# Cumulated decays by chunk in DRAM, a product over its factor, and a second buffer for the backward rows

## The chip, the cores and the metric

The kernel runs on one core of one Trainium2 chip. Its time is the device time of one execution in microseconds: 3032.32 us, median of 3 runs from 3030.61 to 3033.17.

## What is computed

Two network blocks on a sequence of 1024 tokens of width 1024, all in float32. The first is a Mamba-2 block that runs in both directions, with a Fourier mixer beside it; the second is attention and a mixture of experts. The change touches only the chunked scan of the first block. The reference for one direction, with 4 groups of 6 heads, 64 channels a head, a state of 128 and 8 chunks of 128 tokens:

```python
a_cum = jnp.cumsum(a, axis=-1)                 # per head, within a chunk
lmat = jnp.exp(segsum(a))
cb = jnp.einsum('bclgn,bcsgn->bgcls', cc, bc)
y_diag = jnp.einsum('bgcls,bgrcls,bcsgrp->bclgrp', cb, lmat, xc)
decay_states = jnp.exp(a_cum[..., -1:] - a_cum)
states = jnp.einsum('bcsgn,bgrcs,bcsgrp->bcgrpn', bc, decay_states, xc)
...
new_states = jnp.einsum('bgrzc,bcgrpn->bzgrpn', decay_chunk, states)
y_off = jnp.einsum('bclgn,bcgrpn,bgrcl->bclgrp', cc, prev_states, jnp.exp(a_cum))
y = (y_diag + y_off).reshape(bsz, length, g, r, p)
```

The scan runs once forward and once over the flipped sequence, and both results are added.

## The kernel before

Early on, the 48 cumulated decays (24 heads, two directions) of all 1024 tokens are laid out with heads on partitions in `prs` [48, 1024]. ScalarE's queue writes them to DRAM as `pr_d`, and their exponentials as `ep_d` (L418 to L420). From there SyncE's queue later loads single heads' rows broadcast over partitions.

`ssd_group(g)` does one group of heads, chunk by chunk. For chunk step i it calls `off` for both directions and `diag`:

- `off(dr, i)`: TensorE multiplies the carried state H with C into `pof`; VectorE multiplies that by the broadcast decays `er` (two DMAs of 64 partitions x 3 rows x 128 tokens, L757) into `tm` (L763); GpSimd adds `tm` to the output `xs` (L766). Then H is brought forward: `pst` on TensorE (L771), a multiply on GpSimd (L773), an add on VectorE (L775).
- `diag(c)`: `pcb` = B C on TensorE, masked into `cbm`. Two broadcast loads of 6 rows x 128 tokens to 128 partitions, `pf` with the forward rows (L787) and `rb` with the backward rows (L788; the trace calls its tile `rbw`). For each of the 6 heads ScalarE adds a column to `rb` (L791) and VectorE makes the smaller of the two exponents into `pf` (the STT of L792). ScalarE takes the exponential (L794), VectorE the products `W` with the masks (L797), TensorE the products `pd` (L804), and VectorE adds `pd` to `xs` (L807). That add ends a chunk.

Tiles of the pool `wk` have two buffers unless told otherwise. `rb` has one (`bufs=1`), `pf` two. Four PSUM banks (`ps`) serve `pof`, `pst`, `pcb` and `pd`.

The order on each engine is not the order of the code. A planner places instructions by priorities and its own estimates of their durations. The projections of the next group (`plain_tile`, L350, whose PSUM tiles are `pxz`) have a lower priority (`high_priority(-FILL)`) and fill TensorE where the planner sees it wait; in group 3 output products (`out_group`) do that. Each engine executes its own list strictly in order, and a DMA is issued when its turn on its queue has come and its waits are over.

Of the kernel before, what the change touches and what calls it, by code (L numbers as in the profile page):

```python
# [8 lines left out]
F32 = mybir.dt.float32  # L9
# [5 lines left out]
ALU = mybir.AluOpType  # L15
# [4 lines left out]
P = 128  # L20
D = 1024
NT = 8
# [155 lines left out]
def block1(tc, A, x1_d, mod_d, second):  # L178


    nc = tc.nc
    es0 = ExitStack()
    con = es0.enter_context(tc.tile_pool(name="b1c", bufs=1))
    dpool = es0.enter_context(tc.tile_pool(name="b1d", bufs=1, space=DRAM))
# [1 line left out]
    z_d = [dpool.tile([P, 1024], F32, name=f"z{m}") for m in range(16)]  # L186
    u_d = [dpool.tile([P, 1024], F32, name=f"u{m}") for m in range(4)]
    y_d = [dpool.tile([P, 1024], F32, name=f"y{m}") for m in range(16)]
    pr_d = dpool.tile([48, 1024], F32, name="pr_d")
    ep_d = dpool.tile([48, 1024], F32, name="ep_d")  # L190
    hs_d = [[dpool.tile([P, 384], F32, name=f"hs{dr}{g}") for g in range(4)] for dr in range(2)]
    gate_d = dpool.tile([2, 512], F32, name="gate_d")

# [33 lines left out]
    with ExitStack() as e1:  # L227
# [3 lines left out]
        wk = e1.enter_context(tc.tile_pool(name="b1wk", bufs=2))  # L231
# [130 lines left out]
    with ExitStack() as e1:  # L362
# [49 lines left out]
        prs = sp.tile([48, 1024], F32, name="prs")  # L412
        for half in range(2):
# [1 line left out]
            for t in range(4):  # L415
                nc.tensor.transpose(pq[:48, t * P:(t + 1) * P], prt[:, half * 4 + t, :], ident)
            nc.scalar.copy(prs[:, half * 512:half * 512 + 512], pq[:48])
        nc.scalar.dma_start(pr_d, prs)  # L418
        nc.scalar.activation(prs, prs, AF.Exp)
        nc.scalar.dma_start(ep_d, prs)  # L420
        edt.close()


# [264 lines left out]
    with ExitStack() as e2:  # L688
        gp = e2.enter_context(tc.tile_pool(name="b1g", bufs=1, reuse_waits="tile"))
        wk = e2.enter_context(tc.tile_pool(name="b1k", bufs=2, reuse_waits="tile"))  # L690
        psa = e2.enter_context(tc.tile_pool(name="b1qa", bufs=1, space=PSUM))

        def ps1(name):
            return psa.tile([P, 512], F32, name=name, tag="ps", bufs=4)
# [9 lines left out]
        def ssd_group(g):  # L704
# [10 lines left out]
            def by_head(t_):  # L715
                return t_.rearrange("p (h d) -> p h d", d=64)
# [10 lines left out]
            def scaled(c, w, tag, eng):  # L727
                o = wk.tile([P, 6, 64], F32, name=f"xw{g}{c}{tag}", tag="xw", bufs=4)
                eng.tensor_tensor(out=o, in0=by_head(xtok[:, c, :]), in1=w.unsqueeze(2).to_broadcast([P, 6, 64]),
                                  op=ALU.mult)  # L730
                return o
# [18 lines left out]
            def off(dr, i):  # L750

                c = i if dr == 0 else NT - 1 - i
                hs = slice(dr * 24 + 6 * g, dr * 24 + 6 * g + 6)
                er = wk.tile([P, 3, P], F32, name=f"er{g}{dr}{i}", tag=f"er{dr}")
                for q in range(2):
                    rows = ep_d[hs, c * P:(c + 1) * P].rearrange("(j q) t -> q j t", q=2)[q:q + 1]
                    nc.sync.dma_start(er[64 * q:64 * q + 64], rows.broadcast_to([64, 3, P]))  # L757
                po = ps1(f"pof{g}{dr}{c}")
                for j in range(3):
                    nc.tensor.matmul(po[:, j * P:(j + 1) * P], H[dr][:, j * P:(j + 1) * P], ct[:, c * P:(c + 1) * P],  # L760
                                     start=True, stop=True)
                tm = wk.tile([P, 3, P], F32, name=f"tm{g}{dr}{c}", tag="tm")
                nc.vector.tensor_tensor(out=tm, in0=po[:, :384].rearrange("p (j t) -> p j t", j=3),  # L763
                                        in1=er, op=ALU.mult)
                y = xs[:, :, c * P:(c + 1) * P]
                nc.gpsimd.tensor_tensor(out=y, in0=y, in1=tm, op=ALU.add)  # L766
                if i == NT - 1:
                    return
                xw = scaled(c, wS[:, c, hs], f"s{dr}", nc.vector)
                pst = ps1(f"pst{g}{dr}{c}")  # L770
                nc.tensor.matmul(pst[:, :384], btok[:, c, :], xw.rearrange("p h d -> p (h d)"), start=True, stop=True)  # L771
                nx = wk.tile([P, 384], F32, name=f"H{g}{dr}{c}", tag=f"H{dr}")
                nc.gpsimd.tensor_tensor(out=by_head(nx), in0=by_head(H[dr]),  # L773
                                        in1=expT[:, c, hs].unsqueeze(2).to_broadcast([P, 6, 64]), op=ALU.mult)
                nc.vector.tensor_tensor(out=nx, in0=pst[:, :384], in1=nx, op=ALU.add)  # L775
                H[dr] = nx

            def diag(c):
                cs = slice(c * P, (c + 1) * P)
                pcb = ps1(f"pcb{g}{c}")  # L780
                nc.tensor.matmul(pcb[:, :P], bt[:, cs], ct[:, cs], start=True, stop=True)
                cbm = wk.tile([P, 2, P], F32, name=f"cbm{g}{c}", tag="cbm")
                nc.vector.tensor_tensor(out=cbm[:, 0, :], in0=pcb[:, :P], in1=upper, op=ALU.mult)
                nc.vector.tensor_tensor(out=cbm[:, 1, :], in0=pcb[:, :P], in1=lower, op=ALU.mult)
                pf = wk.tile([P, 6, P], F32, name=f"pf{g}{c}", tag="pf")
                rb = wk.tile([P, 6, P], F32, name=f"rbw{g}{c}", tag="rbw", bufs=1)
                nc.sync.dma_start(pf, pr_d[6 * g:6 * g + 6, cs].unsqueeze(0).to_broadcast([P, 6, P]))  # L787
                nc.sync.dma_start(rb, pr_d[24 + 6 * g:30 + 6 * g, cs].unsqueeze(0).to_broadcast([P, 6, P]))  # L788
                for hh in range(6):
                    h = 6 * g + hh  # L790
                    nc.scalar.activation(rb[:, hh, :], rb[:, hh, :], AF.Identity, bias=nrt[:, c, h:h + 1])  # L791
                    nc.vector.scalar_tensor_tensor(pf[:, hh, :], pf[:, hh, :], prt[:, c, h:h + 1], rb[:, hh, :],  # L792
                                                   op0=ALU.subtract, op1=ALU.min)
                nc.scalar.activation(pf, pf, AF.Exp)  # L794
                W = wk.tile([P, 2, 6, P], F32, name=f"W{g}{c}", tag="W")
                for dr in range(2):
                    nc.vector.tensor_tensor(out=W[:, dr], in0=pf, in1=cbm[:, dr, :].unsqueeze(1).to_broadcast([P, 6, P]),  # L797
                                            op=ALU.mult)
                xd = [scaled(c, dtt[:, c, dr * 24 + 6 * g:dr * 24 + 6 * g + 6], f"d{dr}", nc.vector) for dr in range(2)]
                pd = ps1(f"pd{g}{c}")  # L800
                for j in range(3):
                    for dr in range(2):
                        for q in range(2):
                            nc.tensor.matmul(pd[64 * q:64 * q + 64, j * P:(j + 1) * P], xd[dr][:, 2 * j + q, :],  # L804
                                             W[:, dr, 2 * j + q, :], start=(dr == 0), stop=(dr == 1))
                y = xs[:, :, cs]
                nc.vector.tensor_tensor(out=y, in0=pd[:, :384].rearrange("p (j t) -> p j t", j=3), in1=y, op=ALU.add)  # L807

            for i in range(NT):
                if 1 < i < 5:  # L810
                    load_z(i - 2)
                off(0, i)
                off(1, i)
                diag(i)
# [45 lines left out]
    with ExitStack() as e2:  # L860
# [18 lines left out]
        for k in (2, 3):  # L879
            zt[k] = []  # L880
            for n in range(2):
                h, l = (second.h_tile(s, 4 + 2 * (k - 2) + n).rearrange("p k t -> p (k t)") for s in "hl")
# [15 lines left out]
        wk = e2.enter_context(tc.tile_pool(name="b1fin", bufs=4, side="right", reuse_waits="tile"))  # L898
# [1317 lines left out]
def whole(tc, A, out):  # L2216

    nc = tc.nc
    with ExitStack() as e:
        dp = e.enter_context(tc.tile_pool(name="wd", bufs=1, space=DRAM))  # L2220
        x1_d = dp.tile([1024, D], F32, name="x1_d")
        mod_d = dp.tile([12, 512], F32, name="mod_d")
        with tc.tile_pool(name="wz", bufs=1) as zp:
            z = zp.tile([P, D], F32, name="zero_rows")
            nc.gpsimd.memset(z, 0.0)
            nc.gpsimd.dma_start(out[1024:], z)
        second = Second(tc, A, x1_d, mod_d, out, {})
        block1(tc, A, x1_d, mod_d, second)
        with tc.using_default_side("right"):
            second.projections()  # L2230
            attention(second)
            merge(second)
            experts(second)
# [17 lines left out]
```

## Time and profile before

| | |
|---|---|
| median of 3 runs | 3032.32 us |
| the profiled execution | 3029.96 us |
| its span, first to last instruction | 3028.2 us |
| TensorE, VectorE, ScalarE, GpSimd busy | 2710.3, 2115.3, 1484.0, 590.6 us |
| granted TensorE clock, mean | 0.954 |
| the scan (er first issued, last add into xs) | 420.9 to 956.3 us |

The first 95 us hold norms and modulation, up to 410 us the projections and the convolution run, then the scan of four groups to about 960 us. Output products, Fourier part, attention and experts follow, the experts at 370 GB/s of weights. In the scan no engine is full: TensorE is busy for 448.3 of the 550 us from 410 to 960, VectorE for 336.4, ScalarE for 216.3, GpSimd for 160.2. Chunk k of group g carries the number gk in tile names, as `W15`; `er104` is group 1, direction 0, step 4.

### The profile page before, as it was taken

The page shows a single profiled execution, that of the slowest core. Times are in us where ns is not written, and L with a number is a line of the kernel's source. Part 1 is how long each engine was busy: PE and PEld are TensorE (multiplying, and loading weights), DVE is VectorE, ACT ScalarE, POOL GpSimd, SP SyncE. Part 2 cuts the span into 40 slices and gives each one's busy share as a digit, 9 for nine tenths or more (in the row PEclk, how much of TensorE's full clock was granted, in tenths as well). Part 3 has the DMA queues.
Part 4 walks back from the last instruction along what each step waited for, and adds up shares of the span by engine and source line. Part 5 has one row for each costly group of instructions (what it writes and reads, how often), then busy time and mean ns, then how long its engine had stood idle before and what let it go on. Part 6 is the DMA issues. An engine that isn't in the chain of part 4 may idle for free. (4 is left out here: it accounts for less than half of the span.)

```text
span 3028.2 us, 39461 instructions
## 1 busy us (share of the span) xinstructions
PE 2710.3 (90%) x14016; PEld 2135.6 (71%) x14016; DVE 2115.3 (70%) x3664; ACT 1484.0 (49%) x2401; POOL 590.6 (20%) x449
## 2 busy tenths in 40 slices
PE   5999988879787999688999999999999699999997
PEld 2767766657665777566877877778778588777775
DVE  6777747676566656777667745655446899999996
ACT  4433324435342232555766635654221477777774
POOL 2000003222225422421213100000124212112111
PEclk9999998999888999798999999999999799999999
DMA  5265346666545424211233355100445699999995
GB/s 215 78 252 213 125 154 144 192 142 180 137 124 169 154 70 137 91 46 35 81 108 123 111 173 185 47 29 27 139 145 193 230 376 372 368 371 372 373 368 193
DMA packets 270819, 533.08 MB, mean 176 GB/s; under 512 B 25446, under 2 KB 135654, under 8 KB 266524
## 3 DMA queue, kind: packets, MB, share of 16 engines
q1 hardware_dynamic: 202112, 411.98, 40.2%
q10 hardware_dynamic: 56844, 84.99, 7.9%
q0 software_dynamic: 11664, 33.57, 4.5%
q8 instruction: 111, 1.82, 0.2%
q14 instruction: 88, 0.72, 0.1%
HBM read 449.25 MB, written 90.11 MB: 178 GB/s over the span
## 5 line engine op out<-in xcount | busy, mean ns | idle before, releaser
L2057 DVE TENSOR_TENSOR wh<-we,wh 128x1024 fp32r<-128x1024 f32 x390 | 456.2, 1218 | 16.4 <-ACT wh L2054 9.4
L2054 ACT CAST wh<-we 128x1024 fp32r<-128x1024 f32 x396 | 396.6, 1051 | 91.0 <-DMA we<-in_w_ex 28.7
L446 DVE SCALAR_TENSOR_TENSOR acc<-img,cvw,acc 128x945 f32<-128x945 f32 (+2 forms) x160 | 193.1, 1219 | 52.6 <-ACT acc L437 50.6
L2093 PE MATMUL pae<-wh,xle 128*128 128x512 f32 x528 | 207.5, 394 | 5.9 <-DVE xle L2078 5.9
L2091 PE MATMUL pae<-wh,xhe 128*128 128x512 f32 x528 | 210.7, 399 | 2.2 <-ACT xhe L2077 2.2
L2092 PE MATMUL pae<-wh,xhe 128*128 128x512 f32 x528 | 209.8, 397 | 0.1
L792 DVE SCALAR_TENSOR_TENSOR pf<-pf,prt,rbw 128x128 f32<-128x128 f32 x192 | 77.1, 445 | 122.5 <-ACT rbw L791 87.9
L791 ACT ACTIVATE rbw<-rbw,nrt 128x128 f32<-128x128 f32 x192 | 60.0, 390 | 179.0 <-DMA rbw<-pr_d 178.0
L773 POOL TENSOR_TENSOR H<-H,expT 128x384 f32<-128x384 f32 x56 | 54.8, 980 | 455.3 <-DMA H<-hs 348.0
L2114 PE MATMUL pye<-wh,ghe 128*128 128x512 f32 x264 | 106.9, 405 | 21.8 <-ACT ghe L2106 21.8
L350 PE MATMUL pxz<-hTh,w_h 128*128 128x512 f32 x320 | 115.2, 431 | 9.0 <-ACT w_h L143 5.3
L2068 POOL DMA_INDIRECT xg<-h_d,gidx x33 | 35.9, 1089 | 443.3 <-PE pxe L2074 426.2
L350 PE MATMUL pxz<-hTh,w_l 128*128 128x512 f32 x320 | 115.8, 435 | 7.2 <-DVE w_l L144 7.2
L2093 PEld LDWEIGHTS pae<-wh,xle 128*128 128x128 f32 x528 | 99.8, 189 | 27.0 <-DVE xle L2078 6.7
L766 POOL TENSOR_TENSOR xs<-xs,tm 128x384 f32<-128x384 f32 x64 | 74.1, 1161 | 218.6 <-DVE tm L763 218.3
L2091 PEld LDWEIGHTS pae<-wh,xhe 128*128 128x128 f32 x528 | 99.9, 189 | 23.1 <-ACT xhe L2077 2.8
L2092 PEld LDWEIGHTS pae<-wh,xhe 128*128 128x128 f32 x528 | 100.0, 189 | 22.1 <-DVE wh L2057 1.9
L350 PE MATMUL pxz<-hTl,w_h 128*128 128x512 f32 x320 | 111.1, 426 | 0.0
L350 PE MATMUL pxc<-hTh,w_h 128*128 128x512 f32 x320 | 105.8, 404 | 2.6 <-ACT acc L437 2.6
L588 PE MATMUL po<-woh,yh 128*128 128x512 f32 x224 | 92.7, 414 | 14.5 <-DVE acc L593 10.7
L2116 PE MATMUL pye<-wh,gle 128*128 128x512 f32 x264 | 103.7, 393 | 0.1
L2115 PE MATMUL pye<-wh,ghe 128*128 128x512 f32 x264 | 103.1, 391 | 0.0
(911 smaller groups left out, 7687.2 us busy)
## 6 DMA issues: line engine op xcount, KB each, us to landing
we<-in_w_ex SPq DMA_DIRECT2D x396, 512.0 KB
ad_w<-in_ada_w SPq DMA_DIRECT2D x24, 1024.0 KB
wr<-in_w_in SPq DMA_DIRECT2D x40, 512.0 KB
er<-ep_d SPq DMA_DIRECT2D x128, 96.0 KB
pf<-pr_d SPq DMA_DIRECT2D x32, 384.0 KB
rbw<-pr_d SPq DMA_DIRECT2D x32, 384.0 KB
xbc<-acc ACTq DMA_DIRECT2D x20, 512.0 KB
wada<-in_w_ada SPq DMA_DIRECT2D x8, 1024.0 KB
```

The lines of the kernel that those rows point to most:

```text
L350: nc.tensor.matmul(px[j], wt[:, k, :mc], ht[:, k, 512 * j:512 * j + 512], start=(k == 0 and n == 0), stop=(k == KD - 1 and n == 2))
L446: nc.vector.scalar_tensor_tensor(o, img[:, r0 + dy:r1 + dy, c0 + dx:c1_ + dx], cvw[:, m, tap:tap + 1], o, op0=ALU.mult, op1=ALU.add)
L588: nc.tensor.matmul(po, yh[:, ts_], wh, start=(k == 0), stop=False)
L792: nc.vector.scalar_tensor_tensor(pf[:, hh, :], pf[:, hh, :], prt[:, c, h:h + 1], rb[:, hh, :], op0=ALU.subtract, op1=ALU.min)
L2054: last["h"] = nc.scalar.copy(h, raw)
L2057: eng.tensor_tensor(out=l, in0=raw, in1=h.bitcast(F32), op=ALU.subtract)
L2091: nc.tensor.matmul(pa, xh[:, kk, :], h[:, cs], start=(kk == 0), stop=False)
L2092: nc.tensor.matmul(pa, xh[:, kk, :], l[:, cs], start=False, stop=False)
L2093: last["mm"] = nc.tensor.matmul(pa, xl[:, kk, :], h[:, cs], start=False, stop=(kk == KD - 1))
L2114: nc.tensor.matmul(o, gh[:, kk, :], h[:, cs], start=(kk == 0), stop=False)
L2115: nc.tensor.matmul(o, gh[:, kk, :], l[:, cs], start=False, stop=False)
L2116: nc.tensor.matmul(o, gl_[:, kk, :], h[:, cs], start=False, stop=(kk == 3))
```

## The change

`pr_d` and `ep_d` are laid out by chunk, [8, 48 x 128], so that the 6 rows of a group, or the 3 that one `er` DMA takes, are one contiguous run. `pr_d` is still written by one DMA, `ep_d` by six (the heads of each parity and pair apart). The loads become two-dimensional patterns; that of the backward rows comes first. The product of L763 is written over `er`, and `tm` is gone. `rb` has the pool's two buffers.

```diff
-    pr_d = dpool.tile([48, 1024], F32, name="pr_d")
-    ep_d = dpool.tile([48, 1024], F32, name="ep_d")
+    pr_d = dpool.tile([NT, 48 * P], F32, name="pr_d")
+    ep_d = dpool.tile([NT, 48 * P], F32, name="ep_d")
...
-        nc.scalar.dma_start(pr_d, prs)
+        nc.scalar.dma_start(pr_d.rearrange("c (p t) -> p c t", t=P), prs.rearrange("p (c t) -> p c t", t=P))
         nc.scalar.activation(prs, prs, AF.Exp)
-        nc.scalar.dma_start(ep_d, prs)
+        for q in range(2):
+            for j in range(3):
+                nc.scalar.dma_start(ep_d.rearrange("c (d s t) -> s d c t", s=6, t=P)[3 * q + j],
+                                    prs[2 * j + q::6, :].rearrange("p (c t) -> p c t", t=P))
...
-                er = wk.tile([P, 3, P], F32, name=f"er{g}{dr}{i}", tag=f"er{dr}")
+                er = wk.tile([P, 3 * P], F32, name=f"er{g}{dr}{i}", tag=f"er{dr}")
                 for q in range(2):
-                    rows = ep_d[hs, c * P:(c + 1) * P].rearrange("(j q) t -> q j t", q=2)[q:q + 1]
-                    nc.sync.dma_start(er[64 * q:64 * q + 64], rows.broadcast_to([64, 3, P]))
+                    lo = (2 * (4 * dr + g) + q) * 3 * P
+                    nc.sync.dma_start(er[64 * q:64 * q + 64], ep_d[c:c + 1, lo:lo + 3 * P].broadcast_to([64, 3 * P]))
...
-                tm = wk.tile([P, 3, P], F32, name=f"tm{g}{dr}{c}", tag="tm")
-                nc.vector.tensor_tensor(out=tm, in0=po[:, :384].rearrange("p (j t) -> p j t", j=3),
-                                        in1=er, op=ALU.mult)
+                nc.vector.tensor_tensor(out=er, in0=po[:, :384], in1=er, op=ALU.mult)
                 y = xs[:, :, c * P:(c + 1) * P]
-                nc.gpsimd.tensor_tensor(out=y, in0=y, in1=tm, op=ALU.add)
+                nc.gpsimd.tensor_tensor(out=y, in0=y, in1=er.rearrange("p (j t) -> p j t", j=3), op=ALU.add)
...
-                rb = wk.tile([P, 6, P], F32, name=f"rbw{g}{c}", tag="rbw", bufs=1)
-                nc.sync.dma_start(pf, pr_d[6 * g:6 * g + 6, cs].unsqueeze(0).to_broadcast([P, 6, P]))
-                nc.sync.dma_start(rb, pr_d[24 + 6 * g:30 + 6 * g, cs].unsqueeze(0).to_broadcast([P, 6, P]))
+                rb = wk.tile([P, 6, P], F32, name=f"rbw{g}{c}", tag="rbw")
+                for dr, dst in ((1, rb), (0, pf)):
+                    lo = (24 * dr + 6 * g) * P
+                    nc.sync.dma_start(dst.rearrange("p h t -> p (h t)"), pr_d[c:c + 1, lo:lo + 6 * P].broadcast_to([P, 6 * P]))
```

The planner makes another order of the whole scan out of it. Three places:

SyncE in group 1, before (rbw14 is the load of the backward rows of chunk 4, er105 and er115 are the decays of chunk step 5):

```order
L787 DMA pf13_4990<-pr_d_127 128x6x128
L757 DMA er104_5030<-ep_d_128 64x3x128 x2
L788 DMA rbw13_4991<-pr_d_127 128x6x128
L757 DMA er114_5047<-ep_d_128 64x3x128 x2
L787 DMA pf14_5069<-pr_d_127 128x6x128
L757 DMA er105_5107<-ep_d_128 64x3x128 x2
L757 DMA er115_5124<-ep_d_128 64x3x128 x2
L788 DMA rbw14_5070<-pr_d_127 128x6x128
L787 DMA pf15_5146<-pr_d_127 128x6x128
L757 DMA er106_5184<-ep_d_128 64x3x128 x2
L757 DMA er116_5201<-ep_d_128 64x3x128 x2
L788 DMA rbw15_5147<-pr_d_127 128x6x128
```

And in the change:

```order
L791 DMA rbw14_5049<-pr_d_127 128x768
L791 DMA pf14_5048<-pr_d_127 128x768
L791 DMA rbw15_5124<-pr_d_127 128x768
L761 DMA er105_5086<-ep_d_128 64x384 x2
L224 DMA wr7_3560<-in_w_in 128x1024
L761 DMA er115_5102<-ep_d_128 64x384 x2
L791 DMA pf15_5123<-pr_d_127 128x768
L761 DMA er106_5161<-ep_d_128 64x384 x2
L761 DMA er116_5177<-ep_d_128 64x384 x2
L791 DMA rbw16_5199<-pr_d_127 128x768
```

Before, rbw15 came behind the er rows of chunk 6; now it comes ahead of those of chunk 5.

VectorE around W15, the two mask products of chunk 5 in group 1, before:

```order
L797 TENSOR_TENSOR W15_5163<-pf15_5146,cbm15_5143 128x768 x2
L729 TENSOR_TENSOR xw11s1_5211<-xtok1_4651,wS_155 128x384
L763 TENSOR_TENSOR tm106_5191<-pof106_5187,er106_5184 128x384
L792 SCALAR_TENSOR_TENSOR pf16_5223<-pf16_5223,prt_157,rbw16_5224 128x128 x3
L807 TENSOR_TENSOR xs1_4643<-pd15_5170,xs1_4643 128x3x128
L775 TENSOR_TENSOR H106_5198<-pst106_5196,H106_5198 128x384
```

And in the change:

```order
L800 TENSOR_TENSOR W15_5140<-pf15_5123,cbm15_5120 128x768 x2
L795 SCALAR_TENSOR_TENSOR pf17_5259<-pf17_5259,prt_157,rbw17_5260 128x128 x6
L144 TENSOR_TENSOR w14_l_4325<-wr14_4322,w14_h_4324 128x1024
L810 TENSOR_TENSOR xs1_4632<-pd15_5147,xs1_4632 128x3x128
L733 TENSOR_TENSOR xw16d0_5218<-xtok1_4640,dtt_156 128x384
L733 TENSOR_TENSOR xw16d1_5220<-xtok1_4640,dtt_156 128x384
L766 TENSOR_TENSOR er106_5161<-pof106_5164,er106_5161 128x384
L777 TENSOR_TENSOR H106_5174<-pst106_5172,H106_5174 128x384
```

The six STT behind W15 were those of the next chunk, in pieces; now they are those of the chunk after next, all in front of the add that ends chunk 5.

TensorE between pcb03 and pd03 (chunk 3 of group 0), before; pxz121 and pxz120 are a projection of the next group, and 24 such rows stand there in all:

```order
L771 MATMUL pst014_3954<-xw04s1_3952,btok0_3626 128x384
L781 MATMUL pcb03_3959<-ct0_3619,bt0_3618 128x128
L350 MATMUL pxz121_3252<-hTh_414,w12_h_3247 128x512
L350 MATMUL pxz120_3251<-hTl_415,w12_h_3247 128x512
L350 MATMUL pxz121_3252<-hTl_415,w12_h_3247 128x512
L350 MATMUL pxz120_3251<-hTh_414,w12_l_3248 128x512
```

And in the change:

```order
L773 MATMUL pst014_3951<-xw04s1_3949,btok0_3631 128x384
L783 MATMUL pcb03_3956<-ct0_3624,bt0_3623 128x128
L807 MATMUL pd03_3985<-W03_3978,xw03d0_3981 64x128 x2
L764 MATMUL pof004_4004<-ct0_3624,H003_3937 128x128 x3
L807 MATMUL pd03_3985<-W03_3978,xw03d1_3983 64x128 x2
```

The 24 filling rows are gone from this place and stand later.

## Rows read from the trace of the kernel before

**Rows 1.** Busy time by stretch: engine busy us (instructions), granted clock, DMA share, GB/s
```profile
260.00:410.00 150.00, 144.73 (x733) 109.11 (x733) 115.99 (x117) 53.93 (x92) 0.00 (x0) 0.97 0.41 150
...
410.00:960.00 550.00, 448.30 (x2483) 342.98 (x2483) 336.35 (x648) 216.31 (x414) 160.15 (x139) 0.90 0.59 154
...
460.00:560.00 100.00, 82.86 (x499) 63.27 (x500) 75.44 (x143) 39.80 (x79) 31.40 (x30) 0.93 0.61 136
```

**Rows 2.** Waits of 440 to 960 us: who for whom, total us, times, longest
```profile
ACT rbw L791 <- DMA rbw<-pr_d: 178.0, 29, 11.9
...
DVE pf L792 <- ACT rbw L791: 87.9, 21, 12.8
...
PE pd L804 <- DVE W L797: 27.4, 15, 5.2
...
DVE pf L792 <- DMA pf<-pr_d: 26.1, 4, 7.7
...
PE pst L771 <- DVE xs L807: 14.4, 5, 7.1
...
PE ptx L722 <- ACT btok L725: 12.5, 1, 12.5
```

**Rows 3.** SyncE's timeline: start us, us, line, DMA, count
```profile
445.14 1.13 SPq L788 DMA_DIRECT2D rbw<-pr_d  x1
...
608.38 0.37 SPq L788 DMA_DIRECT2D rbw<-pr_d  x1
...
621.90 0.36 SPq L788 DMA_DIRECT2D rbw<-pr_d  x1
...
874.32 0.36 SPq L787 DMA_DIRECT2D pf<-pr_d  x1
```

**Rows 4.** ScalarE's timeline: start us, us, [idle before, and who ended it]
```profile
455.24 1.28 ACT L791 ACTIVATE rbw<-rbw,nrt 128x128 f32<-128x128 f32 x4 [10.61 <-DMA rbw<-pr_d]
...
459.37 0.48 ACT L724 COPY xtok<-ptx 128x384 f32<-128x384 f32 x1 [0.45 <-ACT oz L701]
...
616.62 1.86 ACT L791 ACTIVATE rbw<-rbw,nrt 128x128 f32<-128x128 f32 x6 [7.36 <-DMA rbw<-pr_d]
...
766.14 1.86 ACT L791 ACTIVATE rbw<-rbw,nrt 128x128 f32<-128x128 f32 x6 [11.90 <-DMA rbw<-pr_d]
```

**Rows 5.** VectorE's timeline, the same columns
```profile
485.65 0.55 DVE L807 TENSOR_TENSOR xs<-pd,xs 128x384 f32<-128x384 f32 x1
...
559.14 0.56 DVE L807 TENSOR_TENSOR xs<-pd,xs 128x384 f32<-128x384 f32 x1 [3.49 <-PE pd L804]
...
620.44 1.44 DVE L792 SCALAR_TENSOR_TENSOR pf<-pf,prt,rbw 128x128 f32<-128x128 f32 x3
...
858.74 0.55 DVE L807 TENSOR_TENSOR xs<-pd,xs 128x384 f32<-128x384 f32 x1
881.22 1.66 DVE L792 SCALAR_TENSOR_TENSOR pf<-pf,prt,rbw 128x128 f32<-128x128 f32 x6 [6.92 <-DMA pf<-pr_d]
...
923.30 0.55 DVE L807 TENSOR_TENSOR xs<-pd,xs 128x384 f32<-128x384 f32 x1
```

**Rows 6.** TensorE's timeline, the same columns
```profile
460.07 0.90 PE L722 MATMUL ptx<-ident,xs 128*128 128x128 f32 x3 [12.53 <-ACT btok L725]
...
609.98 1.05 PE L350 MATMUL pxz<-hTh,w_h 128*128 128x512 f32 x2
...
613.84 0.44 PE L804 MATMUL pd<-W,xw12d 128*64 128x128 f32 x4
...
618.84 0.63 PE L350 MATMUL pxz<-hTh,w_l 128*128 128x512 f32 x2
...
622.02 0.61 PE L350 MATMUL pxz<-hTh,w_h 128*128 128x512 f32 x2
```

**Rows 7.** Instructions of single tensors: ns min/median/max, first and last start us
```profile
L757 SPq DMA_DIRECT2D er<-ep_d x128: 573/603/3272, 420.9 to 926.9; - x128
...
L420 ACTq DMA_DIRECT2D ep_d<-prs x1: 315/315/315, 106.1 to 106.1; - x1
```

## Prediction

> **What bounds the kernel now.** I read the table of stretches first. From 410 to 960 us, where the chunked scan runs, TensorE is busy for 448 of 550 us, VectorE for 336, and the DMA engines are 0.59 busy [rows 1]. Neither compute engine is full, so the waits were next. TensorE's idle time there is mostly VectorE's lateness (the product W 27.4 us, the add into xs 14.4) and one wait of 12.5 us at the start [rows 2]. VectorE in turn waits 87.9 us for ScalarE's rbw and 26.1 us for pf's DMA, and ScalarE waits 178.0 us for rbw's DMA [rows 2]. So the timelines of one chunk came third: SyncE issues rbw at 608.38, ScalarE starts on it at 616.62, VectorE's last read of it ends at 620.44 + 1.44 = 621.88, and SyncE issues the next rbw at 621.90 [rows 3, 4, 5]. With one buffer this is a closed loop: 8.2 us of flight and 5.3 us of use, 13.5 us a chunk. The adds into xs that end each chunk show that the loop paces the light chunks: six intervals from 485.65 to 559.14, 12.25 us each [rows 5]. VectorE's work is shorter: 75.4 us in 460 to 560 us, which holds the eight chunks of group 0, is 9.4 us each [rows 1].
>
> TensorE's own work of a chunk is about 4.8 us: from 613.84 to 618.84 with one filling matmul among it. A filling matmul (the projections of L350) costs 0.227 us at 2.4 GHz (14 from 618.84 to 622.02) and nearly twice that at 1.2 GHz (two in 1.05 us at 609.98, after a pause of TensorE) [rows 6]. So a chunk with some 28 of them is bound by TensorE rather than VectorE. In the order of before there are five chunks with 40 to 51 filling matmuls between the last product of one chunk and that of the next, two in group 2 and three in group 3; I call them heavy. The three intervals from 858.74 to 923.30 are heavy, 21.5 us each [rows 5], though 4.8 + 50 x 0.227 = 16.2 us would do for TensorE: there VectorE also waits for pf, whose flight from 874.32 to 881.22 begins only when W has given the buffer back [rows 3, 5].
>
> **The change part by part.**
> The second rbw buffer opens the loop. SyncE's order in group 1 shows it: rbw15 now stands before the er rows of its own chunk, where it stood behind those of the chunk after. What is late next is VectorE's own work, then pf. The period of a light chunk lies between 9.4 us (VectorE without a gap) and 12.25 us (nothing gained). I take 11.2, since the handing to and fro between TensorE and VectorE (pd, xs, pst, each waiting for the other) stays. A group has 7 intervals, four groups 28; the order of the change has 7 heavy ones, so 21 are light: 21 x (12.25 - 11.2) = 22 us gained, bounds 0 and 60.
>
> The planner moved filling matmuls. In group 0 the 24 before pd03 became none, and group 0 as a whole now has 89 instead of 143 between its first pcb and its last pd. They come back as two more heavy chunks (two in group 1, three in group 2, two in group 3). Each costs its price less 12.25 us. By the bounds of 16.2 and 21.5 us that is 8 to 18 us for both; I take 19 us a heavy chunk, hence 13.5 us lost. They are not free: VectorE's order of the change has all six STT of chunk 17 right behind W15, and the buffer of pf17 is the one that W15 frees, so a flight like that of 6.9 us [rows 3, 5] stands in front of the add that ends chunk 15.
>
> At the start of the scan TensorE waited 12.5 us to 460.07 for ScalarE's copies of the turned tiles; these stood behind rbw01, which was issued at 445.14 behind two zt loads and arrived at 455.24 [rows 3, 4, 6]. Now rbw01 has its own buffer, but ScalarE's order puts three additions of rbw02 before those copies, and rbw02 needs rbw00's buffer. It can be issued a few us earlier, without the second zt ahead of it. Bounds 0 and 9 us (an arrival at 446), taken 5.
>
> In group 2 one rbw was so late that ScalarE stood for 11.9 us to 766.14 and the exponential behind it waited too [rows 4]. With the load a chunk ahead this goes: 10 us gained, bounds 0 and 11.9.
>
> Longer runs: er's rows go from 512 to 1536 bytes, pf's and rbw's from 512 to 3072, and their transfers get shorter. From 260 to 410 us, with longer rows, the DMA engines move 150 GB/s at 0.41 busy, 366 GB/s if full; from 460 to 560 us 136 at 0.61, 223 if full [rows 1]. The bytes of the broadcast rows, 1.15 MB a chunk, are two thirds of that stretch. So of the 8.2 us flight I expect 1 to 2 us to go. This is part of the 11.2 us above: without it I would take 11.5. The Trainium skill speaks against any gain here: "DMA: Bandwidth & Descriptors", section Specifications, gives 512 bytes as the smallest transfer that runs at line rate, by which rows of 512 bytes are as good as longer ones; the two stretches do not agree. By that rule the light period is 11.5 and the sum below comes out at 3015, by the rows at 3009.
>
> What costs nothing: the product over er instead of tm is one VectorE instruction of the same shape. It frees er later, on GpSimd's add instead of VectorE's multiply, but that buffer is asked for again two chunks on; if the cover were gone, SyncE would stand for one GpSimd add. The er issues, 603 ns each for three-row patterns [rows 7], may get cheaper, and SyncE waits more than it works. The six writes of ep_d in place of one cost ScalarE five more issues of 0.315 us, 1.6 us at 106 us, long before the first er at 420.9 [rows 7]; without that cover +1.6 us.
>
> The sum, on the profiled execution's 3029.96 us: - 22 + 13.5 - 5 - 10 = - 23.5, or 3006.5 us. The median of the runs is 2.4 us above that execution, hence 3009 us. I let the saving of the stage pass whole to the end: the order of the later stages is the same in both kernels, and they start when the scan is done.
>
> **Rivals.**
> Slower: pf takes rbw's place. pf has had two buffers all along, but holds each from its load to W, longer than rbw, and the order now asks for it earlier. For it: the 26.1 us of VectorE's waits for it [rows 2], pf17 behind W15. Against it: in most light chunks the reads of pf stand a W further on. If the flight stays at 8 us, the light period stays at 12.25 and the moved filling is not paid for: + 18.5 for two heavy chunks at 21.5, - 10 for group 2, start unchanged, 3038.5 and 3041 on the median. With heavy chunks at that price it decides from a light period of about 12.1 us on.
>
> No change: TensorE, now with less filling in group 0, stands waiting for W at pd03 and its like, and the light chunks take 11.7. 21 x 0.55 = 11.5 gained, 18.5 lost, 7 from the start and group 2: 3030, 3032 on the median. For it: TensorE already waits most for W [rows 2]. Against: that W was itself late by rbw.
>
> Much faster: the light chunks come down to 10 us and the heavy to 16.2 because TensorE pauses less and keeps 2.4 GHz: - 47 + 8 - 9 - 12 = - 60, 2970, or 2972 on the median. Against it: VectorE never ran a chunk of group 0 without gaps, and the new order stacks pf's reads behind W.
>
> **How the numbers follow.** The forecast has 0.48, pf in rbw's place 0.21, no change 0.17, much faster 0.14. The forecast's own range is 2990 to 3025. A measurement of this kernel can tell 0.2%, 6 us, from no change. Faster by more: the forecast and the much faster case, 0.62; within: 0.18; slower: 0.20. The range that leaves out 2 in 10 goes from 2978, most of the way to the much faster case, to 3040, just short of the slower one. Likeliest: 3009.
>
> **What would show it.** Right: ScalarE's wait for rbw's DMA falls from 178 us to under 60, VectorE's wait for rbw from 88 to under 30, rbw is issued a chunk before it is read, and six intervals between adds into xs in group 0 take under 70 us instead of 73.5. The row of 410 to 960 us would show the same TensorE work in less time. Wrong: VectorE's waits for pf's DMA grow from 26 to over 60 us, or the adds into xs of group 0 still come every 12 us, or heavy chunks above 22 us. If the stage ends earlier and the whole does not, the saving was lost behind it.

## The result and the profile after

The changed kernel takes 2948.64 us, median of 4 runs (2940.84 to 2951.1), against 3032.74 us for the kernel before (4 runs): a ratio of 0.9723, 95% interval 0.9705 to 0.9741. That is 84 us less where 23 were forecast, and below the range.

The table of stretches of the changed kernel, with the columns of [rows 1]:

```profile
260.00:410.00 150.00, 145.40 (x754) 110.68 (x752) 115.65 (x118) 57.32 (x98) 0.00 (x0) 0.99 0.41 148
410.00:960.00 550.00, 500.53 (x2807) 386.64 (x2808) 409.55 (x732) 243.03 (x454) 196.93 (x162) 0.96 0.56 185
460.00:560.00 100.00, 86.05 (x569) 67.62 (x569) 90.01 (x170) 51.11 (x98) 39.76 (x36) 0.95 0.59 190
```

From 260 to 410 us the rates are alike, though the work there runs some 4 us later than before (the account of the prediction says why). From 410 to 960 us TensorE is busy for 500 us instead of 448, since later work has moved into the stretch, and the DMA engines carry 185 GB/s instead of 154 at a slightly smaller busy share. From 460 to 560 us they carry 190 instead of 136: the same engines move more for about the same busy time.

Waits from 440 to 960 us in the changed kernel, to be read against [rows 2]:

```profile
ACT rbw L794 <- DMA rbw<-pr_d: 43.7, 18, 4.4
...
PE pd L807 <- DVE W L800: 20.5, 18, 5.5
...
DVE pf L795 <- DMA pf<-pr_d: 15.5, 5, 3.5
...
DVE pf L795 <- ACT rbw L794: 3.9, 2, 2.6
```

ScalarE's wait for rbw fell from 178 to 44 us, VectorE's for rbw from 88 to 4, for pf from 26 to 15. The longest single wait for rbw is 4.4 us instead of 11.9. SyncE's, ScalarE's and VectorE's timelines, one fence each, answer to [rows 3 to 5]:

```profile
571.05 0.33 SPq L791 DMA_DIRECT2D rbw<-pr_d  x1
```

```profile
574.84 0.40 ACT L794 ACTIVATE rbw<-rbw,nrt 128x128 f32<-128x128 f32 x1 [1.29 <-DMA rbw<-pr_d]
```

```profile
462.69 0.55 DVE L810 TENSOR_TENSOR xs<-pd,xs 128x384 f32<-128x384 f32 x1
...
530.36 0.56 DVE L810 TENSOR_TENSOR xs<-pd,xs 128x384 f32<-128x384 f32 x1 [0.34 <-PE pd L807]
...
834.58 1.53 DVE L795 SCALAR_TENSOR_TENSOR pf<-pf,prt,rbw 128x128 f32<-128x128 f32 x5 [3.54 <-DMA pf<-pr_d]
...
874.26 0.56 DVE L810 TENSOR_TENSOR xs<-pd,xs 128x384 f32<-128x384 f32 x1 [2.88 <-PE pd L807]
```

The load issued at 571.05 is read at 574.84, 3.8 us on, where it was 8.2 [rows 3, 4]. Below, "flight" is this distance, from SyncE's issue of rbw to ScalarE's first addition, as the median over those chunks in which ScalarE stood idle for it: 8.0 us before (30 chunks), 4.1 after (21). VectorE's stall for pf in a heavy chunk is 3.54 us instead of 6.92. All 32 adds into xs that end a chunk give the place of the saving:

| us | before | after |
|---|---|---|
| first add | 473.5 | 462.7 |
| the 7 intervals of group 0, 1, 2, 3 | 85.6, 89.4, 112.5, 112.3 | 67.7, 82.9, 90.0, 89.4 |
| the 3 steps between groups | 31.5, 26.8, 24.7 | 27.2, 25.8, 28.7 |
| last add | 956.3 | 874.3 |

The scan ends 82 us earlier and the span is 80.1 us shorter (3028.2 and 2948.1): the saving lies in the scan and passes almost whole to the end, as forecast.

### The profile page after: what moved, and what is told of

The parts are those of the page before. It is cut to its first block, busy times and chain, and to the rows that moved or that the text cites. A ratio compares the mean times of both kernels' runs of the same rounds, so it can differ in the third digit from the quotient of the medians.

```text
span 2948.1 us, 39530 instructions
## 1 busy us (share of the span) xinstructions
PE 2686.4 (91%) x14016; PEld 2119.9 (72%) x14016; DVE 2128.3 (72%) x3664; ACT 1484.9 (50%) x2402; POOL 596.0 (20%) x449
## 5 line engine op out<-in xcount | busy, mean ns | idle before, releaser
L351 PE MATMUL pxz<-hTh,w_l 128*128 128x512 f32 x320 | 109.5, 412 | 0.0
L1751 POOL TENSOR_TENSOR sgl<-sgl 128x512 f32<-128x512 f32 x15 | 19.4, 1293 | 429.5 <-DMA wra<-in_w_pf 364.0
L768 POOL TENSOR_TENSOR xs<-xs,er 128x384 f32<-128x384 f32 x64 | 73.1, 1144 | 157.5 <-DVE er L766 140.5
L1208 PE MATMUL ppg<-hg,h2Th 128*128 128x512 f32 x256 | 102.0, 400 | 0.6 <-ACT re L1360 0.6
L351 PE MATMUL pxc<-hTl,w_h 128*128 128x512 f32 x320 | 102.3, 397 | 0.0
```

Of the source, the lines that this page charges most:

```text
L351: nc.tensor.matmul(px[j], wt[:, k, :mc], ht[:, k, 512 * j:512 * j + 512], start=(k == 0 and n == 0), stop=(k == KD - 1 and n == 2))
L768: nc.gpsimd.tensor_tensor(out=y, in0=y, in1=er.rearrange("p (j t) -> p j t", j=3), op=ALU.add)
L1208: nc.tensor.matmul(pp, hTh[t][:, k, :], h, start=(k == 0), stop=False)
```

## The experiments

Two theories: T1, the second buffer opened the loop of load and use, and the longer runs only help; T2, the new layout halved the flight, so that the loop, 4 us of flight and 5 of use, is shorter than VectorE's work of a chunk and no second buffer is needed.

**The buffer without the layout.** With old tables, `tm` has to go to make room:

```diff
-                rb = wk.tile([P, 6, P], F32, name=f"rbw{g}{c}", tag="rbw", bufs=1)
+                rb = wk.tile([P, 6, P], F32, name=f"rbw{g}{c}", tag="rbw")
...
-                nc.vector.tensor_tensor(out=tm, in0=po[:, :384].rearrange("p (j t) -> p j t", j=3),
+                nc.vector.tensor_tensor(out=er, in0=po[:, :384].rearrange("p (j t) -> p j t", j=3),
```

> The kernel before with two rbw buffers and the product written over er (which makes the room for the second buffer); both DRAM tables keep their old layout, pf is loaded first. T1 (the second buffer opened the loop, the layout only helps): 2950 to 2980 us, the xs additions of a group 10 to 11 us apart, ScalarE's wait on rbw between 440 and 960 us falls from 178 us to under 70. T2 (the longer runs halved the flight and so closed the loop's gap): flights stay at 7 to 8 us, light chunks stay at 11 to 12 us, 3000 to 3030 us.

3006.78 us, ratio 0.9924 (0.9908 to 0.9941): 23 us gained, as T2 has it. The flight is 8.4 us. The waits of its profiled execution, which at 2995.48 us is the fastest of the four:

```profile
ACT rbw L790 <- DMA rbw<-pr_d: 122.4, 21, 11.2
...
DVE pf L791 <- DMA pf<-pr_d: 58.9, 12, 8.6
...
DVE pf L791 <- ACT rbw L790: 13.9, 2, 8.6
```

VectorE waits little for rbw now (13.9 us instead of 87.9), but more for pf: 58.9 us instead of 26.1. The prediction's slower rival names this wait; the kernel is faster all the same.

**The layout without the buffer.** The kernel before with only the diff's lines on `pr_d`, `ep_d` and their loads; one rbw buffer, `tm` kept, pf first. All engines, SyncE among them, keep the order of before, but for the writes of the two tables.

> The kernel before with the two tables kept by chunk and loaded in long runs, and nothing else: one rbw buffer, tm kept, pf loaded first. T1: flight 1 to 2 us shorter and the loop stays closed, 3000 to 3025 us, ScalarE's wait on rbw over 120 us. T2: issue of rbw to its use 3 to 5 us, loop 4 + 5 = 9 us and so under VectorE's work, 2950 to 2975 us, ScalarE's wait on rbw under 80 us.

2946.63 us, ratio 0.9724 (0.9708 to 0.9741), flight 4.0 us:

```profile
ACT rbw L794 <- DMA rbw<-pr_d: 59.3, 22, 5.8
...
DVE pf L795 <- ACT rbw L794: 12.3, 7, 8.0
...
DVE pf L795 <- DMA pf<-pr_d: 7.1, 2, 3.6
```

The layout alone is the whole result. Its order has the five heavy chunks of before and not the change's seven. Its last add comes at 864.1 us, 10 us before that of the changed kernel, and yet the whole takes as long: moving the filling cost nothing that can be seen at the end.

**The change without the buffer.** The changed kernel with `bufs=1` on `rb`.

> The changed kernel with one rbw buffer instead of two (both layouts new, rbw first, product over er). T1: the loop is closed again, 2990 to 3020 us, ScalarE's wait on rbw over 100 us. T2: within 15 us of the changed kernel, 2945 to 2965 us, ScalarE's wait on rbw 45 to 80 us.

2946.12 us, ratio 0.9727 (0.9706 to 0.9749), flight 4.0 us. Over the long-flight table the buffer (with the product and the order that come with it) is worth 23 us, over this one nothing. The stretch of group 0:

```profile
460.00:560.00 100.00, 94.21 (x623) 74.15 (x622) 87.56 (x170) 51.93 (x100) 40.65 (x35) 1.00 0.63 204
```

TensorE, busy for 82.9 of these 100 us before [rows 1], is now busy for 94. That it bounds the stretch is not shown: the changed kernel, just as fast, has it busy for 86. T1 has fallen.

**Which table.** The changed kernel with `pr_d` as before (pf and rbw in runs of 512 B, er in long ones), and with `ep_d` as before (the reverse).

> The changed kernel with pr_d laid out as before: pf and rbw are read in runs of 512 B, still rbw first and with two buffers; er keeps its long runs. T1: 2950 to 2970 us. T2: flights of rbw back to 6 to 8 us; 2990 to 3020 us. Should flights be short here too, then it is the er loads whose shorter time lets pf and rbw through.

> The changed kernel with ep_d laid out as before (one write, er in runs of 512 B); pf and rbw keep their long runs and the second buffer. If the short flight of pf and rbw alone carries the saving: 2945 to 2955 us. If the er loads, which share SyncE's queue and the DMA engines with them, matter as the runs with the old pr_d suggest (the two-buffer kernel with both tables old 3006.8 us, with er's table new 2994.3 us, so 12.5 us): 2955 to 2970 us, and flights of rbw of 4.5 to 6 us.

With the old `pr_d` 2994.25 us (0.9883, 0.9866 to 0.9899) and flight 7.7 us; with the old `ep_d` 2949.4 us (0.9729, 0.9712 to 0.9745) and 5.6 us. The table of pf and rbw carries it: 46 us of loss against 1. Short runs of er do lengthen rbw's flight, as the second expectation for the old `ep_d` has it, and the scan from first to last add then takes 419.1 us instead of 411.6; but that kernel has one write of `ep_d` instead of six, and its scan starts earlier (first add at 457.3 us). The two nearly cancel.

**Length of a run, or place of the rows?** The old `pr_d` has short runs, and the six rows of a load lie 4096 B apart. Padding tells the two apart: runs of 512 B again, but 576 B apart.

```diff
-    pr_d = dpool.tile([NT, 48 * P], F32, name="pr_d")
+    pr_d = dpool.tile([NT, 48, P + 16], F32, name="pr_d")
...
-                    lo = (24 * dr + 6 * g) * P
-                    nc.sync.dma_start(dst.rearrange("p h t -> p (h t)"), pr_d[c:c + 1, lo:lo + 6 * P].broadcast_to([P, 6 * P]))
+                    lo = 24 * dr + 6 * g
+                    nc.sync.dma_start(dst, pr_d[c:c + 1, lo:lo + 6, :P].broadcast_to([P, 6, P]))
```

> The changed kernel with each row of pr_d followed by 64 B of padding: pf and rbw are read in runs of 512 B again, but from rows that lie side by side, and every engine's instructions keep their order. If the run's length decides: flights of 7 to 8 us, 2985 to 3005 us, as with the old pr_d (2994.3 us). If it is where the rows lie in DRAM (4096 B apart in the old table): flights of 4 us, 2945 to 2960 us. If part of the old pr_d's loss was the order that the planner made: 2965 to 2985 us with flights of 7 to 8 us.

> The changed kernel with 64 B of padding behind every three rows of pr_d: pf and rbw are read in two runs of 1536 B a partition instead of one of 3072 B (and the table is written by three DMAs). If flight goes with the number of runs (768 a load 7.7 us, 128 a load 4.1 us): 256 runs give 4.8 us, 2950 to 2965 us. If it goes with bytes and only runs of 512 B are slow: 4.1 us, 2945 to 2955 us.

2949.65 us (0.9716, 0.9688 to 0.9744) with runs of 512 B, 2946.44 (0.9713, 0.9697 to 0.9729) with runs of 1536 B; flights 4.8 and 4.6 us. The runs of 512 B cost 0.7 us of flight and no time that can be seen. So it must be the place, and the same kernel was run with other paddings: only the number in `[NT, 48, ...]` differs, the instructions stand in the same order.

> The changed kernel with each row of pr_d padded to 4096 B: runs of 512 B that start 4096 B apart, as in the old table, in the same order of instructions as with rows 576 B apart (2949.7 us). If it is the distance between rows (4096 B, or their spread over many addresses) that makes the flight long: flights of rbw of 7 to 8 us, 2985 to 3005 us. If the old pr_d lost time in another way (where the whole table lies): 2940 to 2960 us.

> As the run with rows 4096 B apart, but 4160 B apart. If the slow thing is rows at the same offset within 4096 B: flights of 4 to 5 us, 2940 to 2960 us. If it is that six rows lie far from one another: flights of 7 to 8 us, 2985 to 3005 us, as with 4096 B.

> As the run with rows 4096 B apart, but 2048 B apart. If rows at one offset within 4096 B collide, half as many do: flights of 5 to 6 us, 2950 to 2985 us. If only a distance of 4096 B or more is slow, or the collision needs it exactly: 2940 to 2960 us.

> As the run with rows of 512 B 4160 B apart (2981.2 us), but 8256 B apart. If the cost levels off once each row lies in a place of its own: 2975 to 2990 us, flights of 7 to 8 us. If it goes on growing with distance, as from 576 over 2048 to 4160 B: 2995 to 3030 us, flights of 9 us or more.

| rows of a load | us | ratio (interval) | flight us |
|---|---|---|---|
| one run of 3072 B | 2948.6 | 0.9723 (0.9705 to 0.9741) | 4.1 |
| 576 B apart | 2949.7 | 0.9716 (0.9688 to 0.9744) | 4.8 |
| 2048 B | 2960.8 | 0.9757 (0.9728 to 0.9787) | 6.2 |
| 4160 B | 2981.2 | 0.9841 (0.982 to 0.9862) | 7.9 |
| 4096 B | 2994.2 | 0.9882 (0.9861 to 0.9903) | 8.1 |
| 8256 B | 3150.1 | 1.0396 (1.0373 to 1.0419) | 13.4 |

But for 4096 B, which is slower than 4160, the time rises with the distance and does not level off; at 8256 B the kernel is slower than before. Two of these times were not expected: 4160 B falls between both expectations, and 8256 B lies 120 us above the higher one. At 4096 B the time is that of the old table (2994.25), which has the same order of instructions and the same distance but an eighth of the size: the distance is all that was wrong with it, not how much memory the table spans. SyncE's queue in 460 to 560 us (packets, MB, share of 16 engines) with rows 576, 4096 and 8256 B apart, one kernel a fence:

```profile
q1 hardware_dynamic: 16760, 14.64, 51.9%
```

```profile
q1 hardware_dynamic: 15871, 14.01, 62.2%
```

```profile
q1 hardware_dynamic: 10971, 10.34, 74.0%
```

Fewer bytes keep the engines busy for longer. With 8256 B ScalarE's timeline, for the rbw issued at 571.43, and the waits from 440 to 1080 us show it in the kernel:

```profile
583.29 1.86 ACT L794 ACTIVATE rbw<-rbw,nrt 128x128 f32<-128x128 f32 x6 [17.71 <-DMA rbw<-pr_d]
```

```profile
ACT rbw L794 <- DMA rbw<-pr_d: 241.6, 25, 19.6
...
DVE pf L795 <- DMA pf<-pr_d: 186.9, 21, 20.2
```

A run with one jump of 4160 B in a partition's load instead of five (two runs of 1536 B):

> The changed kernel with pf and rbw read in two runs of 1536 B a partition that start 4160 B apart (adjacent runs of 1536 B: 2946.4 us; six runs of 512 B 4160 B apart: 2981.2 us). If the cost goes with the number of jumps between far places (one a partition instead of five): flights of 4.5 to 5.5 us, 2948 to 2960 us. If any jump of that size makes the load slow: flights of 6.5 to 8 us, 2970 to 2985 us.

2952.49 us (0.9735, 0.9715 to 0.9756), flight 4.3 us. One jump costs 6 us (against 2946.4), five cost 32 (against 2949.7), so the loss may go with the number of jumps; but these runs are also longer than 512 B, and no run has one jump with short runs or five with long ones.

**The old table with longer rows.** The kernel before with 16 more elements in each row of both tables, its order untouched:

```diff
-    pr_d = dpool.tile([48, 1024], F32, name="pr_d")
-    ep_d = dpool.tile([48, 1024], F32, name="ep_d")
+    pr_d = dpool.tile([48, 1040], F32, name="pr_d")
+    ep_d = dpool.tile([48, 1040], F32, name="ep_d")
```

> The kernel before with its two tables' rows lengthened from 4096 to 4160 B, and nothing else: old layout by row, one rbw buffer, tm kept, pf first, the same instructions in the same order, runs of 512 B. If the distance of 4096 B is the whole cause: 2945 to 2965 us. If rows far from one another are slow: 3025 to 3040 us. If one buffer and runs of 512 B leave part of the loop closed: 2970 to 3000 us.

3007.88 us (0.9923, 0.9901 to 0.9946), flight 7.1 us, outside all three expectations. With 4160 B in both tables the kernel is 24 us faster than with 4096, and most of the loss stays: distance first, and something of its own at 4096 B. Busy shares don't explain that second part: SyncE's queue keeps the engines busier with 4160 B (72.5% in 460 to 560 us in the changed kernel) than with 4096 B (62.2%), and the kernel is faster.

**Could it be better still?** With one rbw buffer there is room for a third er buffer in each direction, for which SyncE waits 107 us in the changed kernel:

```profile
SPq L761 <- POOL xs L768: 107.4, 56, 6.8
```

> The changed kernel with one rbw buffer, and its room given to a third er buffer in each direction. SyncE waits 107 us in 56 waits of the changed kernel's scan for GpSimd to free er, and pf and rbw are queued behind these. If that holds the scan: 2925 to 2940 us. If TensorE and VectorE, which are 94 and 88 of 100 us busy in the first group with one rbw buffer, are the bound now: 2940 to 2952 us, as with one rbw buffer alone (2946.1 us).

2949.48 us (0.9726, 0.9709 to 0.9742). That wait falls only to 101.5 us and nothing is gained. No version that was run lies clearly under the changed kernel; the new layout with fewer writes of `ep_d` was not tried.

## Why the prediction was wrong

- **The step that failed** is the one on longer runs: "of the 8.2 us flight I expect 1 to 2 us to go". 4 us went, and not because of the runs' length. The prediction compared two stretches, 366 GB/s at full busy with long rows and 223 with short ones [rows 1], and put all of it down to length; the stretches differ as well in how far apart a load's rows lie, and that decides: by the same measure, from 460 to 560 us, the kernel with 512 B rows 576 B apart has 174 GB/s at 0.59, 295 if full, and the changed kernel 190 at 0.59, 322. The Trainium skill's rule ("DMA: Bandwidth & Descriptors", Specifications: 512 bytes run at line rate), which the prediction held against, is borne out where rows lie close: 2949.7 us in runs of 512 B, 2948.6 in one run, with 0.7 us between their flights. Its 3015 us failed all the same, since the change also moved the rows together.
- **The loop** was read rightly for the kernel before, but not what becomes of it: with a flight of 4 us it costs next to nothing, and the second buffer, to which the prediction gave the gain, is worth nothing. In the kernel with the layout alone SyncE still issues rbw right behind the last read of the one before (0.03 us, 29 of 31 times), so load and use still follow one another. But the use takes 7.1 us there in the median, instead of 5.2, and VectorE waits for rbw 12.3 us in all instead of 87.9. Nor does the second buffer bring rbw a chunk ahead, as the prediction has it: in 24 of 32 chunks of the changed kernel ScalarE reads it within 7.3 us of its issue, as at 571.05 and 574.84, since it is issued only when VectorE's reads of the chunk before last have freed its buffer (there at 571.02).
- **Some luck** in the buffer alone: its 23 us are near the 23.5 forecast for the whole change, and its intervals in group 0 are 77.5 / 7 = 11.1 us, where 11.2 were taken. But without longer runs the prediction itself has 11.5 and 3015 us, 17 gained.
- **The sum's terms**, from the adds into xs of the two profiled executions. I call heavy the longest intervals of a group, as many as the order has heavy chunks in it (before: two in group 2, three in group 3; after: two, three, two in groups 1 to 3). Before, 5 heavy of 22.5 and 23 light of 12.5 us; after, 7 of 16.8 and 21 of 10.1. So 21 light chunks gave 21 x 2.4 = 50 us, not 22. The two that became heavy cost 2 x (16.8 - 12.5) = 9 us, not 13.5; that the layout alone, with five heavy chunks, is no faster suggests that even these 9 buy time elsewhere. The five that were heavy before fell by 5.7 us each, 28 us, where the prediction had only the 10 us of one late rbw: it did not ask what a shorter flight does to the stalls for pf and rbw in all of them. In the five chunks that are heavy by their filling VectorE waited 21.0 us for pf and 18.5 for rbw; in the kernel with the layout alone, whose order is the same, 7.1 and 0. The start gave 11 us, not 5, outside its bound of 9; with the buffer alone the first add is at 471.7, 2 us earlier than before, and with the layout alone at 461.3, 12 us earlier, so the layout gave nearly all of it. The steps between groups gave 1. Together 50 - 9 + 28 + 11 + 1 = 81, beside the 82 read.
- **The rivals.** "Much faster", at 2972, had the periods nearly right (10 and 16.2 us), but as a matter of TensorE's pauses. TensorE did pause less (its granted clock from 410 to 960 us is 0.96 instead of 0.90), and what part of the saving that carries the runs do not separate. With 0.14 the rival was thought too unlikely, and its sum kept the five old heavy chunks at their old price. pf in rbw's place is seen in the buffer-only kernel, without deciding.
- **The signs** named in advance: the wait for rbw under 60 us, VectorE's for rbw under 30, and six intervals of group 0 under 70 us (58.6) all came. They can't tell the two theories apart: the kernel without the second buffer shows 59.3, 12.3 and 59.5 us. The fourth, rbw issued a chunk before it is read, did not come, and it alone spoke against the second buffer as the cause. Another that could have told is the flight itself.
- **Costed at nothing:** rightly so for the product over er (one rbw buffer, with it 2946.1 us, without it 2946.6), and the saving passes through the later stages nearly whole. The six writes of ep_d were not free. The prediction gave them 1.6 us at most, covered until the first er. They hold ScalarE's queue for 4.71 us, and TensorE's wait for ScalarE behind them grows from 2.18 to 5.13 us (the first line is the kernel before, the others the changed kernel):

```profile
110.29 0.50 PE L350 MATMUL pxc<-hTh,w_h 128*128 128x512 f32 x1 [2.18 <-ACT acc L437]
```

```profile
105.67 4.71 ACTq L423 DMA_DIRECT2D ep_d<-prs  x6
```

```profile
112.69 0.80 PE L351 MATMUL pxc<-hTh,w_h 128*128 128x512 f32 x1 [5.13 <-ACT acc L441]
```

With one write of ep_d in the changed kernel the wait is 2.18 us again. The cover was taken to last until the first er, but the work in between is not idle: TensorE is busy for 144.7 of the 150 us from 260 to 410 us [rows 1], and the delay, some 4 us, is still there at 410 us. The 11 us of the start are what is left after it.

## What to carry to other kernels

When one DMA gathers several short rows for every partition, look at how far apart these rows lie in DRAM before asking for another buffer: here 512 B rows side by side load nearly like one run (4.8 and 4.1 us), and the same rows 4 KB apart take 8 us. When a change both shortens a flight and adds a buffer against it, work out the loop for each alone: whichever is enough by itself to keep the engine behind it from waiting takes all the gain. And a flight that is shortened is shortened in every stall where it stands, not only in the loop that one is looking at.

## What the runs showed of the hardware

Unexpected was the size of the effect: the same 384 KB in the same 768 runs of 512 B take 4.8 us from issue to use with rows 576 B apart, 7.9 at 4160 and 13.4 at 8256 B. A distance of exactly 4096 B costs the changed kernel 13 us more than 4160 B (2994.2 and 2981.2), and 24 us in the kernel before, where both tables were changed. In the trace's list of DMA packets, from 460 to 560 us, those of 512 B take 27 ns in the median at all these distances, and in the mean 36 ns at 576 B, 63 at 4160 and 112 at 8256: distance makes some packets much longer, not all of them a little. What in the memory system makes far rows slow, and what is special at 4096 B, no run here tells: only `pr_d`'s distances were varied alone, always with 128 partitions reading the same rows, so whether loads that are not broadcast behave alike is not shown.
